# Attention probabilities copied by DMA into fp32r tiles and transposed there one unit later, in a gated encoder layer on one Trainium2 core

## The chip, the core and the metric

The kernel runs on one core of a Trainium2 chip. TensorE (PE) multiplies and transposes into PSUM, VectorE (DVE), ScalarE (ACT) and GpSimd (POOL) do the elementwise work, SyncE (SP) issues the DMAs. The metric is the device time of one execution in microseconds. All data is fp32; where a product of fp32 accuracy is wanted, the kernel splits each operand into a high and a low part of the kind fp32r and adds three products (high x high, high x low, low x high), which below is called a triple product.

## The reference

One encoder layer with three gated branches is applied to a prompt of 1024 tokens and a sample of 512 tokens, with the same weights. Cut to the attention, which the change touches:

```python
h = rms_norm(x, ln_pre)
z = h @ w_in                       # split into pool_in, pool_gate, q, k, v, attn_gate, xq, x_gate, merge_logits
q, k = apply_rope(rms_norm(q), ...), apply_rope(rms_norm(k), ...)

def one_block(qblk):               # 8 heads of 64, 2 key/value heads, all L tokens attended
    s = einsum('bqkgd,bskd->bkgqs', qblk, k) * scale
    p = softmax(s, axis=-1)
    return einsum('bkgqs,bskd->bqkgd', p, v)

# cross attention into 256 memory tokens, 4 heads of 128
s = einsum('blhd,bmhd->bhlm', q, mk) * X_HEAD_DIM ** -0.5
p = softmax(s, axis=-1)
out = einsum('bhlm,bmhd->blhd', p, mv)

branches = (pool_out * silu(pool_gate), attn_out * silu(attn_gate), cross_out * silu(x_gate))
merged = sum(sigmoid(merge_logits[n] + b_merge[n]) * (branches[n] @ w_branch[n]) for n in range(3))
y = x + rms_norm(merged @ w_out, ln_post)
```

## The kernel before

The program computes the projections of the prompt first, then the first part of those of the sample. Then comes the part that matters here: a list of attention units is woven with the rest of the sample's projections. After it follow what is left of these projections, the branches, the output projection and the norm.

**Units.** `attention` makes one unit for each pair of a query tile (128 tokens) and a head: 64 for the prompt (1024 keys), 32 for the sample (512 keys). `cross` makes one unit for each block of 512 tokens and head: 8 for the prompt, 4 for the sample. They run in the order prompt attention, prompt cross, sample attention, sample cross. A unit has four steps:

- `ahead`: loads the queries (or, in `cross`, loads and splits them).
- `scores`: matmuls into a PSUM tile A (`mm`, line 133: two products of 512 columns for each 512 keys, so 4 in the prompt and 2 in the sample; 12 of 256 columns in `cross`). Then the maximum of each row on VectorE (L767, in `cross` L854), the exponential on ScalarE (L769, L858) into an SBUF tile `u`, the reciprocal of the sum on VectorE (L770, L859), and the division in place on GpSimd (L771, L862).
- `turn`: transposes the probabilities in pieces of 128 x 128 (`tr`, line 137) into another PSUM tile A: 8 pieces in the prompt and in `cross`, 4 in the sample. Then it splits them into a high part (ScalarE, L172) and a low part (VectorE, L169).
- `values`: multiplies by the values, into a PSUM tile B: 8 products of 256 columns for each unit of the prompt.

`stream` runs the steps shifted against each other: `scores` of unit i, then `turn` of unit i - LAG, then `values` of unit i - LAG - VLAG, with LAG = VLAG = 2. `ahead` runs two units early.

**Buffers.** There are two PSUM tiles A (2 banks each), shared by scores and transposed tiles, four tiles B, and seven SBUF tiles `u`. Raw weights have three buffers, split weights two pairs.

**The weave.** The fill is `plain`: for each of its weight tiles a load (512 KB), a split (ScalarE, VectorE) and 8 triple products, 24 products of 512 columns. `weave` counts a cost for all that is recorded: 1/2.4 ns for each column of a product, 107 ns for a transpose with the fp32 identity `ident`, 56 ns for one with the fp32r identity `identr`. For each nanosecond of unit cost it records SHARE = 0.66 ns of fill.

**Order.** A scheduler takes the recorded instructions and fixes the order on each engine and on SyncE's DMA queue at build time; `tc.high_priority` moves single steps forward. On the chip each engine runs its list in that order and waits where a semaphore says so. All DMAs of this part are issued by SyncE. The transposes of kind fp32r that exist already are those in `kv_tail` and `q_tail`, of parts that are split.

Of the kernel before, what the change touches and what calls it, by code (L numbers as in the profile page):

```python
# [11 lines left out]
F32 = mybir.dt.float32  # L12
F32R = mybir.dt.float32r
# [5 lines left out]
P = 128  # L19
# [5 lines left out]
NXH, XHD, NMEM = 4, 128, 256  # L25
# [36 lines left out]
def encoder_kernel(ctx: ExitStack, tc, wt, xs, xts, mt, cols, rows, rope, edge, ys):  # L62
    nc = tc.nc
# [27 lines left out]
    def A(dt=F32):  # L91
        return ps.tile([P, 1024], dt, tag="A", bufs=2, name=nm("A"))
# [42 lines left out]
    def tr(out, x, i):  # L135
        cost[0] += 107 if i is ident else 56
        pe.transpose(out, x, i[:])  # L137
# [12 lines left out]
    ident = const.tile([P, P], F32, name="ident")  # L150
    make_identity(nc, ident)
    identr = const.tile([P, P], F32R, name="identr")
# [18 lines left out]
    def split(hi, lo, x):  # L171
        act.activation(hi, x, AF.Copy)  # L172
        lo_of(lo, x, hi)
# [559 lines left out]
    def from_scratch(field, bs, dt=F32):  # L733
# [3 lines left out]
            load(t[:, c * BLK:(c + 1) * BLK], field[c][:, bs])  # L737
        return t

    def attention(b, sc, kt, vt, L):  # L740

        bs = slice(b * BLK, (b + 1) * BLK)
        qd, gd, out = sc["q"], sc["attn_gate"], sc["br1"]
        nch = L // P
        units = [(jp, hd, j) for jp in range(TT // 2) for hd in range(NH) for j in range(2)]
        state = {}

        def ahead(i):
            jp, hd, j = units[i]
            if hd == 0 and j == 0:  # L750
                t = M()
                for x in range(2):
                    load(t[:, x * D:(x + 1) * D].bitcast(F32), qd[b * TT + jp * 2 + x][:])
                state["q", jp] = t

        def scores(i):
            jp, hd, j = units[i]
            g = hd // (NH // NG)
            q = state["q", jp][:, j * D + hd * P:j * D + (hd + 1) * P]
            a = A()  # L760
            for n in range(L // 512):
                ns = slice(n * 512, n * 512 + 512)
                mm(a[:, ns], q, kt[g][0][:, ns], start=True, stop=False)
                mm(a[:, ns], q, kt[g][1][:, ns], start=False, stop=True)
            mx, sm, rc = S(1), S(1), S(1)
            with tc.high_priority(PMAX):
                v.reduce_max(mx[:], a[:, :L], axis=AX.X, negate=True)  # L767
                p = U()
                act.activation(p[:, :L], a[:, :L], AF.Exp, bias=mx[:], accum_out=sm[:])  # L769
            v.reciprocal(rc[:], sm[:])  # L770
            pool.tensor_scalar(p[:, :L], p[:, :L], rc[:], 1.0, op0=ALU.mult, op1=ALU.mult)  # L771
            state[i] = p

        def turn(i):
            jp, hd, j = units[i]
            p = state.pop(i)
            if j == 0:
                t = [M(), M()] if nch == 8 else [M()]
                state["pt", i // 2] = [t[0][:], t[1][:]] if nch == 8 else [t[0][:, :D], t[0][:, D:]]
            pv = [t.rearrange("p (c j n) -> p c j n", c=nch, j=2) for t in state["pt", i // 2]]  # L780
            tp = A()
            for c in range(nch):
                tr(tp[:, c * P:(c + 1) * P], p[:, c * P:(c + 1) * P], ident)
            tv = tp[:, :L].rearrange("p (c n) -> p c n", c=nch)
            with tc.high_priority(PTURN):
                split(pv[0][:, :, j], pv[1][:, :, j], tv)

        def values(i):

            jp, hd, j = units[i]  # L790
            g = hd // (NH // NG)
            if j == 0:
                state["o"] = B()
            o, pts = state["o"], state["pt", i // 2]
            for c in range(j * nch // 2, (j + 1) * nch // 2):
                for s in range(2):
                    mm(o[:, :256], vt[:, c, g].rearrange("p s d -> p (s d)"), pts[s][:, c * 256:(c + 1) * 256],
                       start=(c == 0 and s == 0), stop=(c == nch - 1 and s == 1))
            if j == 0:
                return  # L800
            del state["pt", i // 2]
            r = slice((hd % 2) * 64, (hd % 2) * 64 + 64)
            if hd % 2 == 0:
                state["ot"] = HU(), HU()
            ot, gt = state["ot"]
            c, cs = hd // 2, slice(b * BLK + jp * 256, b * BLK + jp * 256 + 256)
            if hd % 2 == 0:
                load(gt[:, :256], gd[c][:, cs])
            with tc.high_priority(EVAC):
                act.activation(ot[r, :256], o[64:128, :256], AF.Copy)  # L810
                v.tensor_tensor(ot[r, :256], o[0:64, :256], ot[r, :256], op=ALU.add)
            if hd % 2:
                pool.tensor_tensor(ot[:, :256], ot[:, :256], gt[:, :256], op=ALU.mult)
                nc.sync.dma_start(out[c][:, cs], ot[:, :256])

        return [(ahead, scores, turn, values, i) for i in range(len(units))]

    def stream(units):
        n = len(units)
        for i in range(-2, n + LAG + VLAG):  # L820
            for k, lag in enumerate((-2, 0, LAG, LAG + VLAG)):
                if 0 <= i - lag < n:
                    units[i - lag][k](units[i - lag][4])
                    yield

    def cross(b, sc, mkd, mvd):

        bs = slice(b * BLK, (b + 1) * BLK)
        xqd, gd, out = sc["xq"], sc["x_gate"], sc["br2"]
        state = {}  # L830

        def ahead(c):
            xf, xq = HU(), U(F32R)
            load(xf[:], xqd[c][:, bs])
            qh, ql = xq[:, 0:BLK], xq[:, BLK:2 * BLK]
            act.activation(qh, xf[:], AF.Copy, scale=XHD ** -0.5)
            v.scalar_tensor_tensor(ql, xf[:], XHD ** -0.5, qh.bitcast(F32), op0=ALU.mult, op1=ALU.subtract)
            if c == 0:
                for k, src in (("mk", mkd), ("mv", mvd)):
                    t = M()  # L840
                    load(t[:].bitcast(F32), src[:])
                    state[k] = [t[:, i * D:(i + 1) * D] for i in range(2)]
            state["q", c] = qh, ql

        def scores(c):
            mk = state["mk"]
            qh, ql = state.pop(("q", c))
            a = A()
            ms_ = slice(c * NMEM, (c + 1) * NMEM)
            for t in range(TT):  # L850
                ts = slice(t * P, (t + 1) * P)
                mm3(a[:, t * 256:(t + 1) * 256], (qh[:, ts], ql[:, ts]), (mk[0][:, ms_], mk[1][:, ms_]), True, True)
            mx, sm, rc = S(4), S(4), S(4)
            v.reduce_max(mx[:], a[:].rearrange("p (t n) -> p t n", t=TT), axis=AX.X, negate=True)  # L854
            p = U()
            for t in range(TT):
                ns = slice(t * 256, t * 256 + 256)
                act.activation(p[:, ns], a[:, ns], AF.Exp, bias=mx[:, t:t + 1], accum_out=sm[:, t:t + 1])  # L858
            v.reciprocal(rc[:], sm[:])  # L859
            for t in range(TT):  # L860
                ns = slice(t * 256, t * 256 + 256)
                pool.tensor_scalar(p[:, ns], p[:, ns], rc[:, t:t + 1], 1.0, op0=ALU.mult, op1=ALU.mult)  # L862
            state[c] = p

        def turn(c):
            p = state[c]
            tp = A()
            for m in range(2):
                for t in range(TT):
                    tr(tp[:, m * 512 + t * P:m * 512 + (t + 1) * P], p[:, t * 256 + m * P:t * 256 + (m + 1) * P], ident)  # L870
            pt = M()
            split(pt[:, 0:1024], pt[:, 1024:2048], tp[:])
            state[c] = pt

        def values(c):
            pt, mv = state.pop(c), state["mv"]
            o = B()
            for m in range(2):
                s = slice(m * 512 + c * XHD, m * 512 + (c + 1) * XHD)
                mm3(o[:], (mv[0][:, s], mv[1][:, s]), (pt[:, m * 512:(m + 1) * 512], pt[:, 1024 + m * 512:1024 + (m + 1) * 512]), m == 0, m == 1)  # L880
            g = HU()
            load(g[:], gd[c][:, bs])
            with tc.high_priority(EVAC):
                v.tensor_tensor(g[:], o[:], g[:], op=ALU.mult)
            nc.sync.dma_start(out[c][:, bs], g[:])

        return [(ahead, scores, turn, values, c) for c in range(NXH)]

    def branch_parts(field, bs):
        t = from_scratch(field, bs)  # L890
# [143 lines left out]
    units = [u for b in range(2) for u in attention(b, sc, kt, vt, 1024)]  # L1034
# [9 lines left out]

LAG, VLAG, SHARE, LOOK, WAIT = 2, 2, 0.66, 1, 6

AHEAD, EVAC, PMAX, PTURN, LATER = 120, 200, 150, 150, 200

# [89 lines left out]
```

## Time and profile before

| | us |
|---|---|
| median of three runs | 1512.16 |
| lowest, highest | 1507.26, 1512.44 |
| the profiled execution | 1511.38 |
| its span, first to last instruction | 1509.6 |
| TensorE busy | 1462.9 (97% of the span) |
| VectorE, ScalarE, GpSimd busy | 981.2, 709.2, 272.4 |
| the woven part in the span | about 690 to 1164 |

The span is what the views below divide; the time of an execution has 1.8 us around it. Matmuls are pipelined, so a row's duration is longer than the distance to the next one's start, and busy TensorE is not TensorE at its peak; the distances between starts are what counts. Some matmul records can be missing from a trace, a few in a hundred at most.

### The profile page before, as it was taken

Reading aid. Unit: us, or ns where it says so; the run is one execution under the profiler, and the core shown is the slowest. Engines: PE = TensorE matmul, PEld = TensorE weight load, DVE = VectorE, ACT = ScalarE, POOL = GpSimd, SP = SyncE. Lnnn points to the kernel's source line nnn. Section 1 sums busy time; section 2 is a strip of 40 time slices with the busy share of each in tenths; the row PEclk is TensorE's granted clock in tenths of the full one; section 3 lists DMA queues with packets and bytes.
Section 4 is the critical chain, followed back from the end, with each engine's and each line's share of the span. In section 5 each row is a group of like instructions: output and inputs, shape, how many; then the busy total and the mean of one; then the engine's idle time right before and its main releaser. Section 6 shows DMA issues by size and latency. Waiting matters only on the chain.

```text
span 1509.6 us, 19658 instructions
## 1 busy us (share of the span) xinstructions
PE 1462.9 (97%) x7264; PEld 1207.9 (80%) x7264; DVE 981.2 (65%) x1262; ACT 709.2 (47%) x1097; POOL 272.4 (18%) x286
## 2 busy tenths in 40 slices
PE   5999999999999999999999999999989999999998
PEld 3778888888888888887888888888767878888887
DVE  5896586666648564646676676666667664764754
ACT  5354444544434544434565555666666323323332
POOL 0001020110000000301222222233233150150241
PEclk8999999999999999999999999999999999999999
DMA  7333234332323433344322222265326854954952
GB/s 274 100 112 110 84 112 126 106 132 65 127 91 93 155 119 126 112 138 138 91 65 78 96 65 90 81 213 185 126 72 233 313 179 138 338 192 141 337 163 84
DMA packets 88174, 211.37 MB, mean 140 GB/s; under 512 B 9872, under 2 KB 19216, under 8 KB 87312
## 3 DMA queue, kind: packets, MB, share of 16 engines
q1 hardware_dynamic: 88080, 210.14, 42.1%
q8 instruction: 57, 0.93, 0.3%
q14 instruction: 37, 0.30, 0.1%
HBM read 155.57 MB, written 54.53 MB: 139 GB/s over the span
## 4 chain that ended last, share of the span: by engine, by line
PE 83%; issue 4%; ACT 4%; DVE 4%; DMA 2%; POOL 1%; SPq 0%; DVEq 0%; POOLq 0%; ACTq 0%
PE B L133 65%; PE A L133 13%; PE A L137 5%; ACT u L769 1%; DMA hu<-xq 1%; DVE wlo L169 1%; ACT med L172 1%; ACT whi L172 1%; DVE s L767 1%; PE B L137 1%; DMA hu<-merge 1%; POOL med L925 1%; POOL s L196 0%; DVE med L169 0%; DMA med<-q 0%
## 5 line engine op out<-in xcount | busy, mean ns | idle before, releaser
L133 PE MATMUL B<-med,whi 128*128 128x512 f32 x2776 | 870.3, 393 | 1.1 <-ACT hu L359 1.1
L133 PEld LDWEIGHTS B<-med,whi 128*128 128x128 f32 x2776 | 513.5, 188 | 104.5 <-ACT hu L359 2.3
L133 PE MATMUL B<-med,wlo 128*128 128x512 f32 x1388 | 542.6, 391 | 0.7 <-DVE wlo L169 0.7
L172 ACT ACTIVATE whi<-raw 128x1024 fp32r<-128x1024 f32 (+1 forms) x168 | 167.3, 996 | 304.4 <-PE B L133 212.6
L133 PEld LDWEIGHTS B<-med,wlo 128*128 128x128 f32 x1388 | 260.7, 188 | 55.9 <-DVE wlo L169 1.7
L169 DVE TENSOR_TENSOR wlo<-raw,whi 128x1024 fp32r<-128x1024 f32 (+1 forms) x168 | 213.0, 1268 | 139.3 <-ACT whi L172 136.8
L172 ACT ACTIVATE med<-A 128x1024 fp32r<-128x1024 f32 (+1 forms) x108 | 96.9, 897 | 121.3 <-PE A L137 121.1
L771 POOL TENSOR_SCALAR u<-u,s 128x1024 f32<-128x1024 f32 (+1 forms) x96 | 94.6, 985 | 317.0 <-DVE s L770 275.7
L169 DVE TENSOR_TENSOR med<-A,med 128x1024 fp32r<-128x1024 f32 (+1 forms) x109 | 115.7, 1061 | 51.6 <-ACT med L172 50.0
L767 DVE TENSOR_REDUCE s<-A 128x1 f32<-128x1024 f32 (+1 forms) x96 | 100.1, 1043 | 42.7 <-PE A L133 20.8
L192 POOL TENSOR_SCALAR s<-s 128x16 f32<-128x16 f32 (+3 forms) x17 | 6.6, 388 | 671.8 <-DVE s L557 324.6
L769 ACT ACTIVATE u<-A,s 128x1024 f32<-128x1024 f32 (+1 forms) x96 | 93.1, 970 | 46.3 <-DVE s L767 45.8
L137 PE MATMUL A<-ident,u 128*128 128x128 f32 x784 | 107.2, 275 | 4.6 <-DVE med L169 2.1
L137 PEld LDWEIGHTS A<-ident,u 128*128 128x128 f32 x784 | 90.8, 141 | 24.8 <-issue 9.6
L133 PE MATMUL A<-kt,med 128*128 128x512 f32 x320 | 96.5, 415 | 10.0 <-ACT u L769 8.8
L925 POOL TENSOR_TENSOR med<-med,hu 128x512 f32<-128x512 f32 x48 | 77.4, 1625 | 136.1 <-DVE hu L923 136.1
L133 PE MATMUL A<-whi,med 128*128 128x512 f32 (+1 forms) x320 | 92.4, 368 | 0.2 <-ACT hu L954 0.2
L172 ACT ACTIVATE whi<-sum 128x1024 fp32r<-128x1024 f32 x50 | 53.1, 1062 | 64.3 <-PE B L133 62.1
L133 PEld LDWEIGHTS A<-kt,med 128*128 128x128 f32 x320 | 54.4, 190 | 34.2 <-ACT u L769 22.9
L133 PE MATMUL B<-med,vt 128*128 128x256 f32 x512 | 76.1, 288 | 1.4 <-ACT med L172 1.4
L169 DVE TENSOR_TENSOR med<-med,med 128x1024 fp32r<-128x1024 f32 (+1 forms) x50 | 55.5, 1115 | 33.7 <-ACT med L172 29.9
L172 ACT ACTIVATE med<-med 128x1024 fp32r<-128x1024 f32 (+1 forms) x44 | 44.3, 1019 | 68.8 <-POOL med L925 42.6
(173 smaller groups left out, 1567.2 us busy)
## 6 DMA issues: line engine op xcount, KB each, us to landing
raw<-wt SPq DMA_DIRECT2D x168, 512.0 KB, 3.7
merge<-hu SPq DMA_DIRECT2D x72, 256.0 KB, 2.1
hu<-merge SPq DMA_DIRECT2D x72, 256.0 KB, 5.4
med<-br SPq DMA_DIRECT2D x36, 256.0 KB, 5.2
q<-hu SPq DMA_DIRECT2D x24, 256.0 KB, 2.6
br<-hu SPq DMA_DIRECT2D x24, 256.0 KB, 2.5
med<-q SPq DMA_DIRECT2D x12, 512.0 KB, 4.5
med<-xt_prompt SPq DMA_DIRECT2D x4, 1024.0 KB, 13.2
```

The costliest lines, as they stand in the source:

```text
L133: pe.matmul(out, l, r, **k)
L137: pe.transpose(out, x, i[:])
L169: v.tensor_tensor(out, x, hi.bitcast(F32), op=ALU.subtract)
L172: act.activation(hi, x, AF.Copy)
L192: pool.tensor_scalar(ss, ss, EPS, 1.0, op0=ALU.add, op1=ALU.mult)
L767: v.reduce_max(mx[:], a[:, :L], axis=AX.X, negate=True)
L769: act.activation(p[:, :L], a[:, :L], AF.Exp, bias=mx[:], accum_out=sm[:])
L771: pool.tensor_scalar(p[:, :L], p[:, :L], rc[:], 1.0, op0=ALU.mult, op1=ALU.mult)
L925: pool.tensor_tensor(at, at, sg[:], op=ALU.add)
```

## The change

The probabilities of a unit, once divided, are copied by a DMA on SyncE's queue from their `u` tile into another `u` tile whose kind is fp32r (`handed`). This is a fifth step, `hand`, recorded one unit after the scores. The transposes take the copy, with the identity of kind fp32r and into a PSUM tile of that kind; the tile is read as fp32 again by the split. LAG goes from 2 to 3, so transposes come one unit later, and the values too. The cost that `tr` records falls from 107 to 56 ns, so the weave changes.

```diff
+    def handed(p):
+        t = U(F32R)[:, :p.free_size()]
+        nc.sync.dma_start(t.bitcast(F32), p)
+        return t
...
+        def hand(i):
+            state[i] = handed(state[i][:, :L])
...
-            tp = A()
+            tp = A(F32R)
             for c in range(nch):
-                tr(tp[:, c * P:(c + 1) * P], p[:, c * P:(c + 1) * P], ident)
-            tv = tp[:, :L].rearrange("p (c n) -> p c n", c=nch)
+                tr(tp[:, c * P:(c + 1) * P], p[:, c * P:(c + 1) * P], identr)
+            tv = tp[:, :L].bitcast(F32).rearrange("p (c n) -> p c n", c=nch)
...
-            for k, lag in enumerate((-2, 0, LAG, LAG + VLAG)):
+            for k, lag in enumerate((-2, 0, 1, LAG, LAG + VLAG)):
...
+        def hand(c):
+            state[c] = handed(state[c])
...
-LAG, VLAG, SHARE, LOOK, WAIT = 2, 2, 0.66, 1, 6
+LAG, VLAG, SHARE, LOOK, WAIT = 3, 2, 0.66, 1, 6
```

In `cross` the transposes change in the same way. Three places show what the scheduler makes of it. In the rows `A` is a PSUM tile of scores or transposes, `kt` the keys, `u` probabilities, `vt` the values, `B` with `whi` and `wlo` fill.

TensorE in the middle of the prompt's units, before: the end of one unit's fill, then the scores of the unit whose tile is `A_6536`, then transposes.

```order
L133 MATMUL B_6488<-med_4499,whi_6484 128x512 x2
L133 MATMUL B_6488<-med_4499,wlo_6485 128x512
L133 MATMUL A_6536<-kt_653,med_6014 128x512
L133 MATMUL A_6536<-kt_654,med_6014 128x512
L133 MATMUL A_6536<-kt_653,med_6014 128x512
L133 MATMUL A_6536<-kt_654,med_6014 128x512
L137 MATMUL A_6549<-ident,u_6455 128x128 x8
L133 MATMUL B_6488<-med_4502,whi_6484 128x512 x2
```

The same place in the changed kernel, the unit with the tile `A_6415`.

```order
L133 MATMUL B_6526<-med_4493,whi_6522 128x512 x2
L133 MATMUL B_6526<-med_4493,wlo_6523 128x512
L133 MATMUL A_6415<-kt_651,med_5980 128x512
L133 MATMUL A_6415<-kt_652,med_5980 128x512
L133 MATMUL A_6415<-kt_651,med_5980 128x512
L133 MATMUL A_6415<-kt_652,med_5980 128x512
L137 MATMUL A_6449<-identr,u_6333 128x128 x8
L133 MATMUL B_6460<-med_6336,vt_655 128x256
```

Before, the transposed `u_6455` is that of the second unit before; now `u_6333` is the copy of the third unit before. Between scores there stood mostly 6, 6 and 12 fill products, now mostly 2 and 10 in turn (or 7 and 6).

SyncE's queue at a like place, before: weight loads (`raw`), gate loads and stores.

```order
L146 DMA hu_6390<-attn_gate_0_615 128x256
L472 DMA attn_gate_1_4526<-hu_6286 128x512
L814 DMA br_1_3_602<-hu_6191 128x256
L146 DMA raw_6923<-wt 128x1024
L472 DMA attn_gate_2_4527<-hu_6432 128x512
L146 DMA raw_7065<-wt 128x1024
```

Now, with the copies (`u` into `u`).

```order
L743 DMA u_6389<-u_6329 128x1024
L146 DMA hu_6598<-attn_gate_1_616 128x256
L472 DMA attn_gate_1_4526<-hu_6440 128x512
L743 DMA u_6445<-u_6385 128x1024
L146 DMA raw_7207<-wt 128x1024
L823 DMA br_1_0_599<-hu_6410 128x256
L743 DMA u_6482<-u_6424 128x1024
L743 DMA u_6539<-u_6478 128x1024
```

Each copy stands in one queue with the loads and stores; one or two of these lie between two copies, or none.

TensorE at the end of the weave, before: the last cross scores (`A_10159`) and what stands ahead of the last unit's transposes (`A_10244`).

```order
L133 MATMUL A_10159<-med_9929,u_10049 128x256 x12
L137 MATMUL A_10186<-ident,u_10070 128x128 x8
L133 MATMUL B_10154<-med_10035,med_4559 128x256
L133 MATMUL B_10233<-med_10151,med_9931 128x512 x6
L133 MATMUL B_10256<-med_10195,med_9931 128x512
L133 MATMUL B_10273<-med_4493,whi_10269 128x512 x2
L133 MATMUL B_10273<-med_4493,wlo_10270 128x512
L133 MATMUL B_10273<-med_4493,whi_10269 128x512 x2
L133 MATMUL B_10273<-med_4493,wlo_10270 128x512
L133 MATMUL B_10273<-med_4496,whi_10269 128x512
L137 MATMUL A_10221<-ident,u_10113 128x128 x8
L137 MATMUL A_10244<-ident,u_10176 128x128
```

Now, from the scores before the last (`A_10139`) to the first transposes of a cross unit.

```order
L133 MATMUL A_10139<-med_9945,u_10025 128x256 x12
L137 MATMUL A_10168<-identr,u_10056 128x128 x4
L133 MATMUL B_10240<-med_10126,med_4559 128x256
L133 MATMUL A_10184<-med_9945,u_10074 128x256 x12
L137 MATMUL A_10228<-identr,u_10124 128x128 x8
L133 MATMUL B_10240<-med_10126,med_4559 128x256 x7
L133 MATMUL B_10279<-med_10237,med_9947 128x512
L133 MATMUL B_10296<-med_4493,whi_10292 128x512 x2
L133 MATMUL B_10296<-med_4493,wlo_10293 128x512
L133 MATMUL B_10296<-med_4493,whi_10292 128x512 x2
L137 MATMUL A_10247<-identr,u_10166 128x128 x8
```

The last scores now follow those before with little between, and three cross units instead of two are to be transposed behind them before the last one.

## Rows read from the trace of the kernel before

**Rows 1.** Stretches, the woven part: us, busy us of each engine, clock, DMA

```profile
690.00:1164.00 474.00, 457.54 (x2665) 380.34 (x2664) 318.51 (x437) 287.01 (x520) 138.56 (x168) 0.99 0.36 116
```

**Rows 2.** Groups by form, woven part: busy us, mean ns, idle before, releasers

```profile
L137 PE MATMUL A<-ident,u 128*128 128x128 f32 x734 | 99.8, 275 | 4.6 <-DVE med L169 2.1 <-ACT u L769 0.9 <-POOL u L862 0.7
```

**Rows 3.** Chain that ended last, a piece behind the woven part: start, us

```profile
1164.38 50.84 PE B L133 x224
```

**Rows 4.** Timeline of TensorE, eight fp32 transposes: start us, us, what

```profile
769.89 1.03 PE L137 MATMUL A<-ident,u 128*128 128x128 f32 x8
770.68 0.71 PE L133 MATMUL B<-med,whi 128*128 128x512 f32 x2
771.23 0.39 PE L133 MATMUL B<-med,wlo 128*128 128x512 f32 x1
```

**Rows 5.** Timeline of TensorE, transposes of kind fp32r in projection tails

```profile
614.83 0.47 PE L137 MATMUL B<-identr,med 128*128 128x128 f32 x4
615.12 0.69 PE L133 MATMUL B<-med,whi 128*128 128x512 f32 x2
615.66 0.40 PE L133 MATMUL B<-med,wlo 128*128 128x512 f32 x1
...
627.38 0.80 PE L137 MATMUL B<-identr,med 128*128 128x128 f32 x8
628.03 1.06 PE L137 MATMUL A<-ident,med 128*128 128x128 f32 x8
```

**Rows 6.** Timeline of TensorE, scores of prompt units 7, 64; sample units 1, 32

```profile
721.41 1.19 PE L133 MATMUL A<-kt,med 128*128 128x512 f32 x4
...
993.68 1.20 PE L133 MATMUL A<-kt,med 128*128 128x512 f32 x4
...
1046.68 0.63 PE L133 MATMUL A<-kt,med 128*128 128x512 f32 x2
...
1137.44 0.74 PE L133 MATMUL A<-kt,med 128*128 128x512 f32 x2
```

**Rows 7.** Timeline, one prompt unit, scores to next scores

```profile
782.87 1.20 PE L133 MATMUL A<-kt,med 128*128 128x512 f32 x4
...
784.98 1.03 ACT L172 ACTIVATE med<-A 128x1024 fp32r<-128x1024 f32 x1 [2.16 <-PE A L137]
...
785.90 1.11 ACT L769 ACTIVATE u<-A,s 128x1024 f32<-128x1024 f32 x1
...
787.15 0.74 PE L133 MATMUL A<-kt,med 128*128 128x512 f32 x2
...
787.50 1.13 POOL L771 TENSOR_SCALAR u<-u,s 128x1024 f32<-128x1024 f32 x1 [3.16 <-DVE s L770]
```

**Rows 8.** Timeline, one sample unit, scores to next scores

```profile
1087.11 0.72 PE L133 MATMUL A<-kt,med 128*128 128x512 f32 x2
...
1087.66 0.60 PE L137 MATMUL A<-ident,u 128*128 128x128 f32 x4
1088.02 0.47 PE L133 MATMUL B<-med,whi 128*128 128x512 f32 x1
...
1089.62 0.73 PE L133 MATMUL A<-kt,med 128*128 128x512 f32 x2
1089.93 0.69 POOL L771 TENSOR_SCALAR u<-u,s 128x512 f32<-128x512 f32 x1 [1.83 <-DVE s L770]
```

**Rows 9.** Timeline, the last cross unit: its scores, its division on GpSimd

```profile
1154.28 1.68 PE L133 MATMUL A<-med,u 128*128 128x256 f32 x12
...
1161.20 2.36 POOL L862 TENSOR_SCALAR u<-u,s 128x256 f32<-128x256 f32 x4 [1.28 <-DVE s L859]
```

**Rows 10.** DMA issues of the page: count, KB each, median us to landing

```profile
raw<-wt SPq DMA_DIRECT2D x168, 512.0 KB, 3.7
hu<-merge SPq DMA_DIRECT2D x72, 256.0 KB, 5.4
...
med<-xt_prompt SPq DMA_DIRECT2D x4, 1024.0 KB, 13.2
```

More of the change, by code (lines that the diff above doesn't have):

```diff
@@ L814, in values @@
                 nc.sync.dma_start(out[c][:, cs], ot[:, :256])
-        return [(ahead, scores, turn, values, i) for i in range(len(units))]
+        return [(ahead, scores, hand, turn, values, i) for i in range(len(units))]
     def stream(units):
@@ L820, in stream @@
         for i in range(-2, n + LAG + VLAG):
-            for k, lag in enumerate((-2, 0, LAG, LAG + VLAG)):
+            for k, lag in enumerate((-2, 0, 1, LAG, LAG + VLAG)):
                 if 0 <= i - lag < n:
-                    units[i - lag][k](units[i - lag][4])
+                    units[i - lag][k](units[i - lag][5])
                     yield
@@ L863, in scores @@
             state[c] = p
+        def hand(c):
+            state[c] = handed(state[c])
         def turn(c):
             p = state[c]
-            tp = A()
+            tp = A(F32R)
             for m in range(2):
                 for t in range(TT):
-                    tr(tp[:, m * 512 + t * P:m * 512 + (t + 1) * P], p[:, t * 256 + m * P:t * 256 + (m + 1) * P], ident)
+                    tr(tp[:, m * 512 + t * P:m * 512 + (t + 1) * P], p[:, t * 256 + m * P:t * 256 + (m + 1) * P], identr)
             pt = M()
-            split(pt[:, 0:1024], pt[:, 1024:2048], tp[:])
+            split(pt[:, 0:1024], pt[:, 1024:2048], tp[:].bitcast(F32))
             state[c] = pt
@@ L885, in values @@
             nc.sync.dma_start(out[c][:, bs], g[:])
-        return [(ahead, scores, turn, values, c) for c in range(NXH)]
+        return [(ahead, scores, hand, turn, values, c) for c in range(NXH)]
     def branch_parts(field, bs):
```

## The prediction

> **What bounds the kernel now.** I read the stretches first. The change touches only the woven part of the program, 690 to 1164 us of the span, where attention units and background products ("fill") share TensorE. There TensorE is busy 457.5 of 474 us at a granted clock of 0.99, the higher of its two levels nearly throughout; VectorE has 318.5, ScalarE 287.0, GpSimd 138.6 [rows 1]. The other engines have room on average, so the question is what TensorE's own work costs, and what it waits for. The groups by form give the transposes: 734 recorded (736 in the code) of fp32 probabilities [rows 2]. Outside this part products run back to back: 224 matmuls in 50.84 us, 0.227 us each [rows 3]. I use that price for every 512-column product, and half of it for a 256-column one.
>
> A unit of prompt attention has 4 score products, 8 transposes and 8 value products, with fill between. From the seventh unit to the last, 57 units take 993.68 - 721.41 = 272.3 us, 4.78 each [rows 6]. By the program order they hold 7.9 fill products each, so their work is 4 x 0.227 + 0.89 + 8 x 0.114 + 7.9 x 0.227 = 4.5 us. TensorE therefore waits about 0.25 us per unit. The timeline shows for what: scores (782.87), maximum on VectorE, exponential on ScalarE (785.90), and only then the next scores (787.15), 4.28 us in all [rows 7]. The next scores need the PSUM tile that the exponential frees. In this loop the exponential stands behind ScalarE's split of the transposed tile (784.98 for 1.03 us). So the stretch has two limits of about the same size, TensorE's work and this loop. In short units (sample attention) the loop is 1089.62 - 1087.11 = 2.51 us [rows 8].
>
> **The transposes.** Eight fp32 ones: from the first (769.89) to the next product is 0.79 us, and the two products behind take 0.55 where 2 x 0.227 is usual; 0.89 us in all [rows 4]. Transposes of the fp32r kind stand in the tails of the q projection: eight in 0.65 us, four in 0.29, and products behind them also take 0.54 for two [rows 5], so 0.74 for eight. The saving is 0.15 us for eight. For four it is 0.36 [rows 8] against 0.29, 0.07. With 64 + 12 blocks of eight and 32 of four: 76 x 0.15 + 32 x 0.07 = 13.6 us of TensorE. This is the most that the change can remove from TensorE's own work. The helper that records a transpose counts 107 ns for the one kind and 56 for the other, but the rows give 0.79 / 8 = 0.099 and 0.65 / 8 = 0.081 to the next product.
>
> The Trainium skill ("TensorE: Matmul & The Clock Gate", "Back-to-back issue gap") has both figures for 128 columns: 56 ns for isolated matmuls, about 81 when a weight load goes with each. This trace's 0.65 us for eight is the second case. By the first alone the saving would come near the one that the helper counts.
>
> **The fill moves.** The weave pays out fill by the recorded cost, so units that count 8 x 51 ns less draw less fill. By the two orders, 627 fill products stand among the units instead of 742. The 115 others, 26.1 us, run behind them at 0.227 us each. That is no work more or less, but each unit has less to cover its waits with.
>
> **Prompt units.** With 6.6 fill products a unit's own work falls to about 4.05 us, most often 3.85 to 4.1. Now the loop sets the pace. A transposed block that ends 0.15 earlier lets the split and the exponential start 0.15 earlier: 4.28 - 0.15 = 4.13. Against that, VectorE's and ScalarE's splits of fill weights fall into tight units. I bound the loop by 4.13 and 4.28 and take 4.23. Each of the 57 units at the larger of its own work plus 0.1 and 4.23 sums to 245.2 us. The same count for the order before, with 4.28, gives 269.5 where the trace has 272.3, so I add the missing 2.8: 248.0. The 73 fill products that moved cost 16.6 later. 264.6 against 272.3: **-7.7 us** (-11.5 at 4.13, -5.5 at 4.28). This is a little under 57 x 0.15 = 8.6: the stretch keeps its saving but no more.
>
> **Sample units.** 31 units take 1137.44 - 1046.68 = 90.8 us [rows 6]. The loop falls to 2.46. The same count gives 82.3, plus 2.0 that the count of before misses, plus 21 x 0.227 = 4.8 for moved fill: 89.1, **-1.7** (-0.2 if the loop stays as it is).
>
> **First units and cross units of the prompt.** Seven and eight blocks keep 0.15 each: **-2.2**. A bound at zero is as plausible.
>
> **The copy.** Each unit adds a DMA on SyncE's queue, 108 in all (64 + 12 of 512 KB, 32 of 256 KB), waiting for GpSimd's normalisation; the transposes stand one unit later than before. No row shows a copy within SBUF. The nearest is a weight load of the same 512 KB, 3.7 us; the far end is 13.2 us for a megabyte [rows 10]. I take 3.7. Cover: in rows 7 the normalised tile is ready at 787.50 + 1.13 - 782.87 = 5.76 us after the scores began; the transposes stand behind the third next scores, 3 x 4.23 + 1.0 = 13.7 us. That leaves 7.9 us, so the copy costs nothing. In the sample it is 3.51 of 7.9 [rows 8], leaving 4.4 for 256 KB; a load of that size can take 5.4 [rows 10], and then each period would be some 0.2 longer, 31 x 0.24 = 7 us. Behind each copy on SyncE's queue stand weight loads, gate loads and stores. Weight loads run up to three tiles (24 products each) ahead of use, so a few us more hide. The copy also waits until the transposes three units back have freed a tile, which happens 4 us before its data is there. The exponential waits for the copy four units back, since that frees its tile; this is met some 10 us early.
>
> **The end of the weave.** Here the cover is missing. Before, the last cross scores start at 1154.28 and their tile is normalised at 1161.20 + 2.36 = 1163.56, 9.3 us later [rows 9]. Now a copy of 3.7 and its issue (0.3) follow: 13.3. The new order has 9.6 us between (19 half products 2.2, three blocks of transposes 2.2, 23 products of 512 columns 5.2), so TensorE waits 3.7. The last three score groups also stand closer, with 2 to 2.6 us of work between. I add a little for that: **+4** (0 if the earlier stages run ahead, 7 if the groups each wait 2 us).
>
> **Sum.** -7.7 - 1.7 - 2.2 + 4.0 = -7.6. The profiled execution took 1511.38 us (1509.6 of span and 1.8 around it), so 1503.8; it lies 0.8 under the median of 1512.16, which would go to 1504.6. I say 1504.5.
>
> **The rivals.** (a) *The whole saving is kept*: the loop falls to 4.13 and the end hides behind fill: 1511.4 - 11.5 - 1.7 - 2.2 + 1 = 1497. For it speaks that the split does stand before the exponential; against it that units without fill are exactly those with waits. (b) *The loop eats it*: where a fill weight's split comes between scores and maximum, a unit is about a microsecond longer; if that happens every fourth to sixth unit the loop averages 4.4, the sum of units is 253.2 + 2.8 + 16.6 = 272.6, and the stretch gains nothing: 1512. (c) *The copy is late*: slower. A transposed block that waits for its copy holds the scores of the fourth next unit, so four units last 5.76 + landing + 3.0 (the work behind the block). This passes 4 x 4.23 from a landing of 8.1 us on. At 10 us a unit lasts 4.7, 64 x 0.46 = 30 us more: 1534; at 9 us 1519. Against it stands the 3.7 us, for it that copies share SyncE's one queue with stores that wait for fill results, and that the DMA engines get 108 more transfers. (d) *The kind brings no speed* where the data was only relabelled: no gain of 13.6, and the end's wait: 1513. (e) *The counted price is right*: 51 ns less for each of 736 transposes, 37.5 us: 1511.4 - 37.5 + 4 = 1478. Rows 5 speak against it.
>
> **How the numbers follow.** Forecast 0.53 (its own range 1500 to 1510), (a) 0.17, (b) 0.13, (c) 0.11, (d) 0.04, (e) 0.02. A measurement of this kernel can tell about 0.5% (7.6 us) from no change: the line is at 1504.6, in the middle of the forecast. So faster: half of the forecast, (a) and (e), 0.46; within 0.5%: the other half, (b), and most of (d), 0.42; slower: (c) and the rest, 0.12. The range from 1496 to 1514 leaves out (c), (e) and a little at both ends.
>
> **What would show it.** Right: fp32r blocks of eight at about 0.65 us to the next product; scores to scores of 4.1 to 4.3 us in tight units, ended by the exponential; about 26 us more of unbroken fill behind the last unit; a wait for a DMA before the last transposes and hardly elsewhere. Wrong: copies that land later than 8 us, waits for DMA before transposes in each unit (c), blocks as long as before (d), or periods of 4.4 and more with VectorE's weight split before the maximum (b).

## The result, and the profile after

The changed kernel takes 1502.5 us (median of seven) where the kernel before takes 1512.1 on the same chip: ratio 0.9948, 95% interval 0.9932 to 0.9964, some 8 us less by the ratio and 9.6 by the medians. One of the seven executions ran at a granted clock of 0.56 and took 2376 us; the six others lie between 1500.7 and 1504.2, and the ratio is theirs. The forecast was 1504.5. The profiled execution took 1501.9 us, 1500.1 of it span, against 1511.4 and 1509.6. The total was close, but two of its terms were far off and cancelled, as the stages show.

The rows that answer to [rows 6] are the score products of prompt units 7 and 64 and of sample units 1 and 32 (timeline of TensorE: start us, us, what):

```profile
720.05 1.20 PE L133 MATMUL A<-kt,med 128*128 128x512 f32 x4
...
961.15 1.20 PE L133 MATMUL A<-kt,med 128*128 128x512 f32 x4 [0.19 <-ACT u L775]
...
1010.90 0.73 PE L133 MATMUL A<-kt,med 128*128 128x512 f32 x2
...
1100.18 0.66 PE L133 MATMUL A<-kt,med 128*128 128x512 f32 x2
```

With the first scores and the last transposes of the weave they give the stages below. "Moved" is the fill that left a stage for the part behind the weave, at 0.227 us a product; the net is after less before, plus moved.

| stage | before, us | after, us | moved | net | forecast |
|---|---|---|---|---|---|
| first scores to prompt unit 7 | 25.9 | 24.1 | 1.6 | -0.2 | -1.0 |
| 57 prompt units | 272.3 | 241.1 | 16.6 | **-14.6** | **-7.7** |
| prompt unit 64 and 8 cross units | 53.0 | 49.8 | 1.6 | -1.7 | -1.2 |
| 31 sample units | 90.8 | 89.3 | 4.8 | **+3.3** | **-1.7** |
| last sample unit to last transposes | 26.7 | 30.3 | 1.6 | +5.2 | +4.0 |
| all | | | 26.1 | -7.9 | -7.6 |

Another 1.8 us went behind the weave, between the first two output phases (111.2 us before, 109.4 after), in code that the change doesn't touch. Every kernel below with less fill in the weave has 109.3 to 109.8 there, the two that have as much as before 110.3 and 110.6; the cause is open.

One prompt unit of after, as [rows 7] showed one of before (timeline: start us, us, engine, line, what, and the idle time before it with what ended it):

```profile
804.45 1.20 PE L133 MATMUL A<-kt,med 128*128 128x512 f32 x4
...
805.48 0.80 PE L137 MATMUL A<-identr,u 128*128 128x128 f32 x8
...
806.31 1.03 ACT L172 ACTIVATE med<-A 128x1024 fp32r<-128x1024 f32 x1 [1.51 <-PE A L137]
...
807.24 1.11 ACT L775 ACTIVATE u<-A,s 128x1024 f32<-128x1024 f32 x1
...
808.48 0.78 PEld L133 LDWEIGHTS A<-kt,med 128*128 128x128 f32 x4 [0.16 <-ACT u L775]
...
808.61 1.09 PE L133 MATMUL A<-kt,med 128*128 128x512 f32 x4
```

The weights of the next scores load 4.03 us after the scores began; in the unit of [rows 7] their products started after 4.28. (Here a fill product stands between, so the products start after 4.16.) The split on ScalarE starts 1.86 us after the scores instead of 2.11; from the split on all is as long as before, and the next scores still wait for the exponential. So the loop still sets the pace and became 0.25 us shorter. Of the 57 periods from scores to scores 47 are under 4.4 us, with a median of 4.10; before, 27 are, with a median of 4.22.

Five of the 57 units are held up as rival (b) said: the split of a fill weight stands in front of the maximum on VectorE.

```profile
883.99 1.21 PE L133 MATMUL A<-kt,med 128*128 128x512 f32 x4
...
885.05 1.42 DVE L169 TENSOR_TENSOR wlo<-raw,whi 128x1024 fp32r<-128x1024 f32 x1 [0.88 <-ACT whi L172]
...
886.40 1.21 DVE L773 TENSOR_REDUCE s<-A 128x1 f32<-128x1024 f32 x1
...
888.95 1.20 PE L133 MATMUL A<-kt,med 128*128 128x512 f32 x4
```

These five last 5.09 us on average, the 52 others 4.15, all together 4.23.

The sample units show the loss. The stretches of one of their bad places (from and to, us, busy us of TensorE, its weight loads, VectorE, ScalarE and GpSimd, granted clock, DMA share, GB/s):

```profile
1052.00:1058.00 6.00, 6.00 (x39) 5.06 (x38) 4.23 (x9) 3.58 (x9) 2.22 (x4) 1.00 0.88 283
1058.00:1062.00 4.00, 2.04 (x12) 1.48 (x12) 3.09 (x6) 3.93 (x9) 1.83 (x2) 1.00 0.63 231
1062.00:1065.40 3.40, 3.35 (x15) 2.77 (x14) 2.27 (x6) 1.48 (x5) 1.51 (x3) 0.50 0.55 106
```

The timeline there, with one block of transposes ahead of it:

```profile
1057.00 0.46 PE L137 MATMUL A<-identr,u 128*128 128x128 f32 x4
...
1059.64 0.69 DVE L773 TENSOR_REDUCE s<-A 128x1 f32<-128x512 f32 x1 [0.69 <-PE A L133]
1059.77 1.06 ACT L172 ACTIVATE whi<-raw 128x1024 fp32r<-128x1024 f32 x1
1060.85 0.69 ACT L775 ACTIVATE u<-A,s 128x512 f32<-128x512 f32 x1
...
1061.68 0.95 PE L133 MATMUL A<-kt,med 128*128 128x512 f32 x2 [1.83 <-ACT u L775]
...
1062.89 0.75 PE L137 MATMUL A<-identr,u 128*128 128x128 f32 x4
```

A fill weight's split (1059.77) stands ahead of the exponential on ScalarE and holds it up by 0.52 us: the maximum is done at 1060.33, the exponential starts at 1060.85. TensorE has no fill left to bridge the whole and waits 1.83 us. In the 3.4 us behind the wait the granted clock is 0.50, the lower level (1.2 GHz), and four transposes take 0.75 us instead of 0.46. It happens twice in these units (again from 1041.5 us on). The 31 sample units as one stretch, before and after:

```profile
1046.68:1137.44 90.76, 83.85 (x469) 66.40 (x467) 61.52 (x116) 54.77 (x117) 28.32 (x39) 1.00 0.39 128
1010.90:1100.18 89.28, 80.13 (x444) 62.98 (x444) 61.89 (x117) 54.31 (x116) 27.99 (x40) 0.96 0.63 211
```

TensorE is idle 9.2 us instead of 6.9, and the mean clock is 0.96 instead of 1.00. Waits for the exponential are not new here: before, TensorE has four, of 5.0 us in all.

The end, which answers to [rows 9] (timeline, with SyncE's queue):

```profile
1121.27 0.47 SPq L743 DMA_DIRECT2D u<-u  x1
...
1127.59 0.84 PE L137 MATMUL A<-identr,u 128*128 128x128 f32 x8 [1.72 <-DMA u<-u]
```

It is the only wait of TensorE that the trace puts down to a copy. The block is the last but one. Its copy, issued at 1121.27, lands at 1127.45, after 6.2 us, twice the median. The copy of the last block, issued at 1125.77, lands at 1129.62, 0.3 us before that block starts. The lines of the page for transposes and copies, against [rows 2] and [rows 10]:

```profile
L137 PE MATMUL A<-identr,u 128*128 128x128 f32 x736 | 76.7, 245 | 4.3 <-DMA u<-u 1.7
...
u<-u SPq DMA_DIRECT2D x76, 512.0 KB, 3.2
...
u<-u SPq DMA_DIRECT2D x32, 256.0 KB, 2.6
```

### The profile page after: what moved, and what is told of

Same layout as the page of the kernel before. It is cut to its first block, busy times and chain, and to the rows that moved or that the text cites. A ratio compares the mean times of both kernels' runs of the same rounds, so it can differ in the third digit from the quotient of the medians.

```text
span 1500.1 us, 19878 instructions
## 1 busy us (share of the span) xinstructions
PE 1449.7 (97%) x7264; PEld 1196.4 (80%) x7264; DVE 982.6 (66%) x1262; ACT 710.7 (47%) x1097; POOL 271.8 (18%) x286
## 5 line engine op out<-in xcount | busy, mean ns | idle before, releaser
L137 PEld LDWEIGHTS A<-identr,u 128*128 128x128 f32 x736 | 74.5, 142 | 20.1 <-issue 4.9
L137 PE MATMUL A<-identr,u 128*128 128x128 f32 x736 | 76.7, 245 | 4.3 <-DMA u<-u 1.7
L169 DVE TENSOR_TENSOR wlo<-sum,whi 128x1024 fp32r<-128x1024 f32 x50 | 61.1, 1222 | 23.2 <-ACT whi L172 22.3
```

Source lines behind the costliest of these rows:

```text
L169: v.tensor_tensor(out, x, hi.bitcast(F32), op=ALU.subtract)
```

## The experiments

The change has four parts: the kind, the copy, the later transposes (lag 3) and the thinner weave (unit transposes recorded at 56). **Theory:** the kind makes the gain, in the prompt units' loop; lag, copy and thin weave give some of it back. **Rival:** the later transposes or the thinner weave make the gain, and the kind is idle.

Each ratio is to the kernel before on the same chip; the chips are not the same in all rows, so the ratios compare better than the medians.

| kernel | us, median | ratio to before, 95% interval |
|---|---|---|
| the change | 1502.5 | 0.9948 [0.9932, 0.9964] |
| thinner weave alone | 1511.9 | 0.9998 [0.9989, 1.0007] |
| lag 3 alone | 1513.6 | 1.0010 [1.0000, 1.0021] |
| thinner weave and lag 3 | 1515.4 | 1.0025 [1.0013, 1.0036] |
| the same with fp32 copies | 1522.5 | 1.0067 [1.0054, 1.0079] |
| the change, weave as before | 1505.6 | 0.9958 [0.9945, 0.9971] |
| kind and thinner weave alone | 1495.6 | 0.9887 [0.9872, 0.9902] |
| the change at lag 2 | 1579.0 | 1.0438 [1.0417, 1.0460] |
| the change, each copy twice | 1595.6 | 1.0549 [1.0532, 1.0565] |
| copies from GpSimd's queue | 1552.9 | 1.0276 [1.0259, 1.0293] |
| cross units not copied | 1501.6 | 0.9944 [0.9925, 0.9963] |
| prompt units alone copied | 1500.2 | 0.9926 [0.9912, 0.9940] |
| the same, other units' weave as before | 1495.5 | 0.9894 [0.9877, 0.9912] |

The traces give the stages of each kernel as above. Below, each stage is taken net of its fill, at 0.227 us a product, and against the kernel before (us; a minus is a gain):

| kernel | 57 prompt units | unit 64, cross | 31 sample units | end |
|---|---|---|---|---|
| the change | -14.6 | -1.7 | +3.3 | +5.2 |
| thinner weave alone | +0.5 | -2.3 | +3.9 | -0.5 |
| lag 3 alone | +1.2 | -0.4 | +1.4 | +2.8 |
| thinner weave and lag 3 | -0.3 | -1.4 | +6.7 | +2.4 |
| the same with fp32 copies | -0.5 | +1.2 | +6.8 | +7.3 |
| the change, weave as before | -12.9 | +3.0 | +0.8 | +6.8 |
| kind and thinner weave alone | -13.8 | -2.2 | +4.8 | +1.1 |
| cross units not copied | -14.9 | -0.1 | +2.0 | +3.6 |
| prompt units alone copied | -14.7 | +2.1 | +4.0 | -0.4 |
| the same, other units' weave as before | -14.8 | +0.4 | +0.8 | 0.0 |

**Everything but the kind.**

```diff
-        t = U(F32R)[:, :p.free_size()]
-        nc.sync.dma_start(t.bitcast(F32), p)
+        t = U()[:, :p.free_size()]
+        nc.sync.dma_start(t, p)
...
-            tp = A(F32R)
+            tp = A()
```

(and `ident` for `identr` in the two `turn` functions, still recorded at 56).

> The changed kernel with its copies, its lag of 3 and its thinner weave, but copies and transposes of the fp32 kind (unit transposes still recorded at 56 ns). Theory (the kind is the gain: 0.15 us for each block of eight, and the loop shortened by as much): all of the 13.6 us of TensorE comes back, 64 prompt units at about 4.38 instead of 4.23, sample units 0.07 longer: 1513 to 1517 us, ratio to the kernel before 1.000 to 1.003. Rival (the gain comes from the later transposes and the thinner weave, the kind is nearly idle): 1501 to 1505, ratio 0.995.

1522.5 us: 20 us over the change, and over the 1513 to 1517 expected. The kind is what gains, more than the theory said. A prompt unit of this kernel beside the one of after shown above:

```profile
803.83 1.12 PE L133 MATMUL A<-kt,med 128*128 128x512 f32 x4
804.79 1.04 PE L137 MATMUL A<-ident,u 128*128 128x128 f32 x8
805.86 1.02 ACT L172 ACTIVATE med<-A 128x1024 fp32r<-128x1024 f32 x1 [2.15 <-PE A L137]
806.79 1.11 ACT L775 ACTIVATE u<-A,s 128x1024 f32<-128x1024 f32 x1
...
808.04 1.20 PE L133 MATMUL A<-kt,med 128*128 128x512 f32 x4
```

From the first transpose to the split it is 1.07 us, with fp32r 0.83 (806.31 - 805.48). These are also the medians over the 57 prompt units of both kernels. To the next product a block differs by only 0.79 - 0.63 = 0.16. The loop hangs on the split, which needs the last transposed piece, and that comes 0.24 us earlier. The 57 prompt units take 255.9 us here and 241.1 in the change: 0.26 each. The kind also gains 3.5 us in the sample units (+6.8 against +3.3). The orders of the two programs are much alike: 79 and 85 of the 108 blocks of transposes stand directly behind scores.

**Thinner weave alone, lag 3 alone, and both.**

The thinner weave, in the kernel before:

```diff
-                tr(tp[:, c * P:(c + 1) * P], p[:, c * P:(c + 1) * P], ident)
+                tr(tp[:, c * P:(c + 1) * P], p[:, c * P:(c + 1) * P], ident, 56)
```

The later transposes, in the kernel before:

```diff
-LAG, VLAG, SHARE, LOOK, WAIT = 2, 2, 0.66, 1, 6
+LAG, VLAG, SHARE, LOOK, WAIT = 3, 2, 0.66, 1, 6
```

> The kernel before with one thing changed: the unit transposes are recorded at 56 ns instead of 107, so that some 115 fill products leave the weave and run behind it. No copy, no fp32r, lag 2. Theory (the kind is the gain): the prompt units fall to about 4.35 by having less work, and the moved fill costs 26 us behind; net 1508 to 1513, ratio 0.998 to 1.001. Rival (the thinner weave is the gain): 1501 to 1506, ratio 0.995.

> The kernel before with the transposes one unit later (lag 3 instead of 2), nothing else. Theory (the kind is the gain): the transposes never waited for their tile by much, so nothing in the loop moves; the end may lose 1 to 2 us with one more unit in flight: 1510 to 1515, ratio 0.999 to 1.002. Rival (the lag is the gain, since it takes waits of the transposes away): 1502 to 1506, ratio 0.995.

> The kernel before with the thinner weave (unit transposes recorded at 56) and a lag of 3, no copy, fp32 transposes: what the first experiment has without the copies. Theory (the later lag costs in the thinner weave, where sample units and the end have less fill to cover it): 1517 to 1522, close to the fp32 copies at 1522.5. Rival (the copies themselves cost the 10 us that separate the fp32 copies from the thinner weave alone): 1511 to 1514.

1511.9, 1513.6 and 1515.4 us. None of the parts without the kind gains: the rival is out. Moving fill is worth nothing by itself in the prompt units: they shorten by 16.7 us, and the 76 fill products that left them are 17.3. In the sample units it costs: they last as long as before with 17 products less, 3.9 us lost net. Their row:

```profile
1020.99:1111.83 90.84, 81.90 (x451) 63.68 (x451) 63.90 (x119) 54.95 (x118) 26.86 (x40) 1.00 0.38 121
```

TensorE idles 8.9 us in it, nearly as in the change, at a clock of 1.00: the loss comes without a drop of the clock.

Lag 3 alone costs little, and with the thinner weave some 3.5 us, between what the two readings expected; the sample units last 93.6 us there, against 90.8 at lag 2 with the same 120 fill products, and the end 28.6 against 25.8 with the same 36:

```profile
1111.83:1137.59 25.76, 24.37 (x152) 20.33 (x152) 16.58 (x26) 18.02 (x50) 11.94 (x20) 1.00 0.54 182
1113.26:1141.90 28.64, 25.82 (x164) 21.87 (x165) 18.95 (x30) 19.11 (x51) 10.93 (x20) 1.00 0.64 217
```

The first is lag 2, the second lag 3, neither with a copy. From 1515.4 to the 1522.5 of the first experiment the fp32 copies cost 7 us. The two profiles differ most in the units before prompt unit 7 (25.0 us against 21.4), in the cross units (51.9 against 47.3, of which 2.0 are nine more fill products) and at the end (32.4 against 28.6).

**The change with the weave as before.**

```diff
-                tr(tp[:, c * P:(c + 1) * P], p[:, c * P:(c + 1) * P], identr)
+                tr(tp[:, c * P:(c + 1) * P], p[:, c * P:(c + 1) * P], identr, 107)
```

> The changed kernel with the unit transposes recorded at 107 ns as before, so that the weave draws as much fill as before. Theory (the kind is the gain and the thin fill costs at the end and in the sample units): prompt units at about 4.6 instead of 4.78 with 7.9 fill products, sample units 0.05 to 0.07 shorter than before, the end of the weave with more cover: 1498 to 1504, ratio 0.990 to 0.995. Rival (the thinner weave is the gain): back at the time before, 1509 to 1513, ratio 0.999.

1505.6 us, just over the 1498 to 1504 expected: the kind gains without the thin weave too, 14.1 us in the prompt units against lag 3 alone (258.0 and 272.1). More fill was to help behind them, and in the sample units it does: 93.6 us with 30 more products than in the change is 2.5 us less net. The cross units (55.1 us) and the end (34.9) are longer than in the change, by 4.7 and 1.6 us net. From prompt unit 64 on TensorE idles 16.6 of 183.5 us, at a mean clock of 0.95.

**The kind without copy and lag.**

```diff
+            p, e = U(F32R), p
-            pool.tensor_scalar(p[:, :L], p[:, :L], rc[:], 1.0, op0=ALU.mult, op1=ALU.mult)
+            pool.tensor_scalar(p[:, :L], e[:, :L], rc[:], 1.0, op0=ALU.mult, op1=ALU.mult)
```

> No copy and a lag of 2: GpSimd's normalisation writes its product into a second tile of the fp32r kind (so the probabilities are rounded to that kind, a lower precision than the kernel before has), and the transposes are fp32r, counted at 56. Theory (the kind is worth some 15 us in the prompt units and 2 in the sample units, and copy and lag cost 8 to 10): 1491 to 1497, ratio 0.987 to 0.990. Rival (copy and lag are free): 1500 to 1504, as the changed kernel.

1495.6 us, as the theory said. It is 16 us below the thinner weave alone: the kind without copy and lag. (The product also goes to a second tile instead of being made in place; what that does by itself was not tested.) By the medians the change keeps 9.6 us of this and gives some 7 to copy and lag. The prompt units take 241.2 us, the same as in the change: there the copy costs nothing. The woven part shows 3 of the 7 us: 4.1 more at the end, 1.1 less in the other stages. Another 3.1 us lies ahead of it in these two executions (first scores at 692.8 and 695.9 us), where no unit runs yet; its cause is open, so copy and lag cost between 3 and 7 us.

**How far is the copy from being late?** Lag 2 (`LAG` of the change set to 2), each copy made twice (a loop of two around the `dma_start`), and copies from GpSimd's queue (`nc.gpsimd.dma_start`):

> The changed kernel with its transposes back at a lag of 2, so that the copy has one unit less of cover. The normalised tile of a prompt unit is ready some 5.7 us after its scores start, the copy lands at about 5.7 + 0.3 + 3.2 = 9.2; the transposes would stand at 2 x 4.1 + 1.0 = 9.2. In the sample 3.5 + 0.3 + 2.6 = 6.4 against about 2 x 2.7 + 0.8 = 6.2. Theory (the copy is just as long as its issue row says and the later lag costs some 8 us in sample units and at the end): prompt units 0 to 0.2 us longer, sample units and end a few us shorter: 1498 to 1510. Rival (copies land later than their row says, behind stores and loads on SyncE's queue): waits for the copy in each unit, 1515 to 1535.

> The changed kernel with each copy made twice, the second behind the first, into the same tile. Theory (the copy is hidden in prompt units by 3 to 4 us, in sample units and at the end by less): prompt units land at 5.7 + 0.6 + 6.4 = 12.7 against 13.0, hardly a wait; sample units at 3.5 + 0.6 + 5.2 = 9.3 against 7.9 to 8.5, some 0.3 longer each, 5 to 10 us; the end 3 to 6 us: 1508 to 1518. Rival (copies have plenty of cover everywhere, since no unit of the changed kernel waits for one): 1501 to 1506. Second rival (the DMA engines are the cost, whatever the cover): prompt units 0.2 and more longer, 1520 and over.

> The changed kernel with its copies issued from GpSimd's queue, right behind the normalisation that they wait for, instead of from SyncE's. Theory (a copy on SyncE's queue holds up hardly anything: half of them are issued 0.03 us after the normalisation ends, and loads behind them come in time): 1500 to 1505. Rival (SyncE's queue, where copies wait for a normalisation ahead of loads and stores, is what copies cost): 1495 to 1498. Second rival (issuing costs GpSimd over a microsecond each time): 1508 and over.

1579.0, 1595.6 and 1552.9 us. All three missed by far. For the first two the waits for copies explain only a part: TensorE's waits before transposes name a copy for 10.7 us of the whole program with lag 2, and for 23.0 us with doubled copies. What also differs is the order of the program. In the change 85 of 108 blocks of transposes stand directly behind scores, with lag 2 only 13, with doubled copies 16 (counted in TensorE's rows of the trace). The order is fixed when the program is built; I take it that other products are put ahead where a copy is reckoned to come late, which was not tested. Rows of the kernel with lag 2:

```profile
809.86 1.20 PE L133 MATMUL A<-kt,med 128*128 128x512 f32 x4
810.90 0.76 PE L133 MATMUL B<-med,vt 128*128 128x256 f32 x5
...
813.80 0.79 PE L137 MATMUL A<-identr,u 128*128 128x128 f32 x8
814.42 1.15 PE L133 MATMUL A<-kt,med 128*128 128x512 f32 x4
...
814.62 1.03 ACT L172 ACTIVATE med<-A 128x1024 fp32r<-128x1024 f32 x1 [0.83 <-PE A L137]
...
816.98 1.12 ACT L775 ACTIVATE u<-A,s 128x1024 f32<-128x1024 f32 x1 [1.33 <-POOL u L777]
```

The block stands 3.94 us behind the scores instead of 1.03, right before the next scores, and the next exponential falls behind the late split. The mean prompt unit takes 5.14 us. How much a lag of 2 would cost with the transposes left in their place was not measured. With GpSimd's queue the order is good (86 of 108), but the copies are issued late: 1.31 us after the normalisation, where SyncE's queue has 0.03 (medians). Groups of its page (busy, mean ns, idle before with its releaser):

```profile
L137 PE MATMUL A<-identr,u 128*128 128x128 f32 x736 | 80.3, 252 | 37.3 <-DMA u<-u 28.9
...
L743 POOL DMA_DIRECT2D u<-u x108 | 65.0, 602 | 174.2 <-issue 134.1
```

Issuing takes GpSimd 0.60 us each and it idles 174.2 us before these; what for, the trace doesn't say. The Trainium skill ("SBUF — State Buffer", "SBUF: two separate sides") states that VectorE's two-port operations can lock GpSimd out while it writes the descriptors of its own DMAs; no run here shows whether that is the cause.

**Where do copies pay?** Cross units without copies (no `handed`, `ident`, at lag 3); then copies, fp32r and lag 3 for the 64 prompt units alone, all other units fp32 at lag 2; then the same with the other units recorded at 107 again.

Prompt units alone copied:

```diff
-            state[i] = handed(state[i][:, :L])
+            if nch == 8:
+                state[i] = handed(state[i][:, :L])
...
-            tp = A(F32R)
+            tp = A(F32R if nch == 8 else F32)
```

The other units' weave as before:

```diff
-                tr(..., identr if nch == 8 else ident, 56)
+                tr(..., identr if nch == 8 else ident)
```

> The changed kernel without copies in the 12 cross units, whose transposes stay fp32 (counted at 56 all the same); attention units, lag 3 and weave as changed. Theory (copies cost where their cover is thin, in the 8 cross units of the prompt, 49.8 us against 46.2 without copies, and at the end, 30.3 against 27.3): these come back, less 12 x 0.16 to 0.24 us of longer blocks: 1497 to 1500. Rival (it is the lag of 3 that costs there, or the copies of the attention units): 1502 to 1506.

> Copies, fp32r and a lag of 3 in the 64 attention units of the prompt alone; cross units and sample units with fp32 transposes, no copy and a lag of 2 (all unit transposes counted at 56, so the weave is as thin as in the changed kernel). Theory (the gain is made in the prompt units, the loss of 7 us from copies and lag elsewhere): 1496 to 1500, from 1502.5 less 7 plus some 2 to 4 for the longer blocks of the other 44 units. Rival (copies cost as much in the prompt units, through the queue and the DMA engines): 1502 to 1506.

> As the kernel with copies in the prompt units alone, but the fp32 transposes of the sample and cross units are recorded at 107 again, so that these units draw as much fill as in the kernel before; prompt units stay at 56. Theory (what the sample units lose, 7 to 9 us of idle TensorE against 1.6 before, comes from the thinner weave): 3 to 5 us come back, 1495 to 1498. Rival (copies or the prompt units' order cost them, whatever the fill): 1499 to 1502, as without the change.

1501.6, 1500.2 and 1495.5 us. The first can't be told from the change: the expectation missed, and the cross units last as long without their copies (49.7 us). Most of the 3.6 us that it wanted back there was fill: the change has 81 products in this stage, the kernel with 46.2 us has 68. The end is 28.7 us, 1.6 less than with copies:

```profile
1100.18:1130.50 30.32, 24.78 (x163) 20.86 (x163) 18.47 (x28) 18.44 (x50) 10.65 (x20) 1.00 0.82 269
1099.49:1128.18 28.69, 24.33 (x159) 20.74 (x159) 18.89 (x29) 18.44 (x50) 10.69 (x20) 1.00 0.78 261
```

The first row is the change. The kernel with the prompt units alone copied has the whole end back (25.8 us), with the copies gone and the lag at 2, but is not surely faster than the change, since the intervals overlap. The third is surely faster, by some 7 us, and its probabilities are copied, not written to the fp32r kind by an engine; what precision the fp32r transposes keep is not measured here. It is 4.7 us below the second, and their intervals just touch; by the stages the sample units give 3.2 us of it and the cross units 1.7. (The idle time before that its expectation gives as 1.6 us is 6.9 in the row of the sample units above.) From prompt unit 64 to the last transposes, one row of each kernel's stretches (columns as above). The kernel before:

```profile
993.68:1164.11 170.43, 161.26 (x949) 132.62 (x948) 117.59 (x189) 111.42 (x263) 58.70 (x92) 1.00 0.48 159
```

The thinner weave alone:

```profile
974.83:1137.59 162.76, 152.38 (x899) 124.19 (x898) 113.81 (x186) 106.03 (x258) 56.24 (x92) 1.00 0.47 152
```

The change:

```profile
961.15:1130.50 169.35, 154.53 (x930) 126.76 (x931) 117.00 (x187) 109.45 (x259) 58.25 (x92) 0.98 0.73 248
```

Prompt units alone copied:

```profile
959.97:1128.07 168.10, 157.76 (x925) 128.15 (x926) 115.93 (x188) 108.81 (x259) 58.88 (x92) 0.99 0.50 165
```

The last kernel:

```profile
959.40:1130.19 170.79, 162.02 (x956) 132.34 (x957) 116.52 (x187) 110.40 (x261) 57.67 (x92) 1.00 0.49 163
```

TensorE is idle 9.2, 10.4, 14.8, 10.3 and 8.8 us in them. The change idles most, and its clock is below 1.00. The last kernel has the fill back, idles as little as before at a clock of 1.00, and takes the stretch's fill off the part behind it (92.4 us from the last transposes to the first output phase, against 98.7 in the change).

## Why the prediction was right in sum, and wrong in its terms

- **Loop of the prompt units (failed).** "A transposed block that ends 0.15 earlier lets the split and the exponential start 0.15 earlier" took the price up to the next product on TensorE. The loop runs through the reader of the tile. Up to the split the saving is 0.24, the loop fell to between 4.03 and 4.10, below the bound of 4.13, and the term was -14.6 instead of -7.7. By estimate 57 x (0.25 - 0.15) = 5.7 of the missing 6.9 us are this price. The 0.10 that the forecast put on the bound for weight splits was not far off: the five held-up units cost 5 x 0.94 = 4.7 us. The measured mean is the 4.23 that the forecast took as the least a unit could last. Read the other way, what it put on top of that, 4.1 us for units with more work of their own and 2.8 carried over from the order before, makes up the 6.9.
- **Sample units (failed).** The same count, the larger of a unit's own work and a loop of 2.46 us (2.51 less the 0.07 saved is rather 2.44), held no room for waits that fill no longer covers. The units lasted 2.88 us on average, 3.3 us lost net where 1.7 were to be gained. The thinner weave alone, with no kind, copy or later lag, loses 3.9 there, and fill at the old rate in the last experiment leaves 0.8 lost where the thin fill leaves 4.0. So moved fill was not free in these units, as the forecast had it.
- **First and cross units.** -2.2 forecast, -1.8 measured.
- **The end (near by luck).** +4 forecast, +5.2 measured. The forecast put a wait of 3.7 us for a copy before the last transposes. The trace has 1.7 us, before the last block but one, whose copy took 6.2 us to land. Without copies in the cross units the end is 1.6 us shorter. The larger part is the later lag, for which the forecast added only "a little": by itself it lengthens the end by 2.9 us (25.8 to 28.6).
- **The copy.** Its cover was right. The copy of a prompt unit is issued 7.7 us before its transposes (median over the units, 7.9 forecast), lands in 3.2 us, and of 108 blocks one has a wait put down to a copy. That "the copy costs nothing" holds in the prompt units; over the whole kernel copies and lag cost 3 to 7 us, of which the traces show the end.
- **Moved fill.** The part from the last transposes to the first output phase grew by 26.0 us (26.1 forecast).
- **The kind.** Blocks of eight take 0.63 us to the next product (0.65 in [rows 5]), which is 79 ns each. The Trainium skill ("TensorE: Matmul & The Clock Gate", "Back-to-back issue gap") gives about 81 where a weight load goes with each; the trace agrees with that and not with its isolated 56.
- **Rivals.** (a) and the forecast shared the truth: the prompt units kept more than the whole saving, the end and the sample units took it back. (b) happened, with its price of about a microsecond (0.94), but in 5 of 57 units and not in every fourth to sixth. (c) did not happen, but one unit less of lag turns the gain into a loss of 67 us, more than (c) had; the waits named a copy are 10.7 of them. (d) and (e) are out: the block takes 0.63 us where fp32 takes 0.79, 79 ns for each transpose and not 56.

## What to carry to other kernels

When a loop runs through several engines, price a faster step up to the moment when its reader can start, not up to the next instruction on its own engine. Work that fills gaps pays differently in each stage: here it was worth nothing in the long units, bound by another loop, and 3 to 4 us in the short ones. A detour by DMA should stand where its cover is longest (here the 64 long units), and the order that the build makes of it must be looked at: at a lag of 2 the kernel lost 67 us, with 13 blocks directly behind scores instead of 85, and the waits for copies are 10.7 of these.

## What the runs showed of the hardware

- From the first of eight transposes to the start of the ScalarE operation that reads them: 1.07 us for fp32, 0.83 for fp32r; to the next product 0.79 and 0.63.
- A copy within SBUF issued on SyncE's queue lands in 3.2 us for 512 KB and 2.6 for 256 KB (medians; 2.3 to 8.1 over all). The Trainium skill ("DMA: Bandwidth & Descriptors", "Anatomy of one DMA — SWDGE (gpsimd) path") has a fit of 2.0 us plus bytes over 436 GB/s for another issue path; the estimate from it, 3.2 and 2.6, agrees.
- Behind a wait of 1.83 us, in a stretch where TensorE was busy 2.04 of 4 us, the granted clock was 0.50 for the next 3.4 us.
- The sample units of the thinner weave alone idle 8.9 us at a mean clock of 1.00, those of the change 9.2 us at 0.96.
- A DMA issued from GpSimd holds that engine for 0.60 us.
